# Loading the expert rows of u: four GpSimd gathers to all 128 partitions in place of four SyncE transfers to 32 partitions each

## The chip, the cores and the metric

The kernel runs on one core of one Trainium2 chip. The metric is the device time of one launch in microseconds (us), taken as the median of three runs. The core has TensorE for matrix products, VectorE (DVE in the profile), ScalarE (ACT), GpSimd (POOL) and SyncE (SP), which only issues transfers. Transfers run on 16 DMA engines, whichever engine issued them.

## The reference, cut to what matters

One decoder layer works on 512 tokens of width 2048. It has a token mixer (a convolution group and a differential attention group) and then a feed-forward part made of 16384 experts with one neuron each. Each token picks 16 experts in each of 8 heads by two scores. The expert part is:

```python
def apply(args):
    xb, ib, gb = args
    u = jnp.take(expert_u, ib, axis=0)
    a = jnp.einsum('thkd,td->thk', u, xb)
    w = (jax.nn.gelu(a.astype(jnp.float32), approximate=False) * gb).astype(xb.dtype)
    vv = jnp.take(expert_v, ib, axis=0)
    return jnp.einsum('thk,thkd->td', w, vv)
```

expert_u and expert_v are 16384 x 2048 in float32, 128 MB each. All else of the layer (projections, attention, the selection of experts) comes before this part.

## The kernel before, in words

The kernel splits the 512 tokens. 352 of them (TD) are computed densely: every expert's activation is computed for every token, and a gate matrix that is zero for experts not chosen is multiplied in. The other 160 (TG) are computed sparsely: for each token the chosen rows of expert_u and expert_v are gathered, one row to a partition.

The dense part runs over 128 blocks of 128 experts. `u_load` (L497 to L500) brings a block of expert_u, 128 rows of 8 KB, into a tile `ur` of 128 partitions by 4 by 512. Partition 32 s + r holds, in place b, the 2 KB segment s of row 32 b + r. It does so by four transfers of SyncE, one for each s, each to 32 partitions. This layout lets VectorE turn the block in squares of 32 by 32 (`utf`, L767, two halves to a block). Each half is split in a rounded part (ScalarE, L88) and a remainder (VectorE, L89) into `ut`, and TensorE multiplies it with the dense tokens (`pa`, L779). `ur` has two buffers (UR_BUFS), `utf` and `ut` two each. The tile is asked for one half-block ahead (AHEAD).

Eight blocks make a chunk. After the u side of a chunk comes its v side, `v_group`: tiles `vr` of expert_v, 512 KB each, loaded by SyncE (L922, three buffers), split by L88 and L89 into `vs`, and multiplied with the gated activations W (`pv`, L932). Results are added into `acc`.

Woven into both sides are the gathers of the sparse part: `gathered` (L829 to L836) issues an indirect DMA of GpSimd (L831) that fetches half a row of 4 KB for each of 128 partitions into `gt` (four buffers, GBUF). VectorE multiplies and sums it (L840 for u, L856 for v). There are 640 gathers. Each also waits for a recent matmul (`pace`), so that the gathers follow TensorE.

A scheduler in the tool chain lays down the order of instructions on each engine at compile time from readiness and program order; at run time each engine works through its own list in order, and the semaphores hold it.

Before the dense part, in the output projection (L505 to L548), the first 12 blocks (NPRE) are loaded by the same `u_load` into `uar` (two buffers), turned and stored in DRAM in turned form, one block to every second step of weights. In that stage GpSimd computes the remainders of the weights (`wsp`, L89 with the engine given as GpSimd). These 12 blocks come back later by plain transfers (L760) that the change doesn't touch. So `u_load` runs 128 times: 12 for `uar`, 116 for `ur`.

Of the kernel before, what the change touches and what calls it, by code (L numbers as in the profile page):

```python
# [14 lines left out]
U32 = mybir.dt.uint32  # L15
# [7 lines left out]
P = 128  # L23
T = 512
D = 2048
# [53 lines left out]
def hymba_peer(tc, x, c, positions, w_ada, b_ada, norm1_g, w_in, conv_w, q_norm_g, k_norm_g,  # L79
               lambda_q1, lambda_k1, lambda_q2, lambda_k2, subln_g, w_out, norm2_g,  # L80
               w_peer_q, sub_keys1, sub_keys2, expert_u, expert_v, out):
    nc = tc.nc
    x, out = x[0], out[0]
    w_ada, w_in, w_out, w_peer_q = w_ada[0], w_in[0], w_out[0], w_peer_q[0]
    expert_u, expert_v = expert_u[0], expert_v[0]
# [12 lines left out]
    with ExitStack() as ctx:  # L98
        const = ctx.enter_context(tc.tile_pool(name="const", bufs=1))
# [6 lines left out]

        ident = const.tile([P, P], F32, name="ident")
        make_identity(nc, ident)
        modc = const.tile([P, 6, KC], F32, name="modc")
        big_ctx = ctx.enter_context(ExitStack())  # L110
        early = big_ctx.enter_context(tc.tile_pool(name="early", bufs=1))
# [23 lines left out]
        def px():  # L135
            return psX.tile([P, T], F32, name="px")
# [358 lines left out]
        x1 = []  # L495

        def u_load(t, e):  # L497
            for s in range(4):
                nc.sync.dma_start(t[s * 32:(s + 1) * 32],
                                  expert_u[e * P:(e + 1) * P, s * 512:(s + 1) * 512].rearrange("(b r) d -> r b d", r=32))  # L500

        def u_quarter(t, ur, q):
            nc.vector.transpose(t, ur[:, :, q * P:(q + 1) * P].rearrange("p b (c r) -> p c b r", r=32))
# [2 lines left out]
        def u_ahead(e):  # L506
            ur = pu.tile([P, 4, 512], F32, name="uar")
            u_load(ur, e)
            t = pu.tile([P, 4, 4, 4, 32], F32, name="uat", bufs=PU_BUFS)
            for q in range(4):  # L510
                u_quarter(t[:, q], ur, q)
            nc.sync.dma_start(u_dram[e], t.rearrange("p q c b r -> p (q c b r)"))
# [3 lines left out]
        for dg in range(4):  # L516
            xr = xy.tile([P, NT, 512], F32, name="xr")
            nc.sync.dma_start(xr, x[:, dg * 512:(dg + 1) * 512].rearrange("(i p) d -> p i d", p=P))
            for j in range(4):
                t = px()  # L520
# [50 lines left out]
        for k in range(KC):  # L571
            xs = x1[k]
            t = nc.vector.scalar_tensor_tensor(xs, xs, a_col[:, 1, k:k + 1], rst, op0=OP.mult, op1=OP.mult)
# [17 lines left out]
        for i, kk in enumerate((sub_keys1, sub_keys2)):  # L591
            kr = tk.tile([P, P], F32, name="kr", bufs=1)
            nc.sync.dma_start(kr, kk[0])
            t = px()
# [158 lines left out]
        def u_turn(n):  # L753
            e, q = divmod(n, 2)
            if e >= NK:
                return
            if q == 0:
                UR[0] = up.tile([P, 4, 512], F32, name="ur", bufs=UR_BUFS)
                if e < NPRE:
                    nc.sync.dma_start(UR[0].rearrange("p b d -> p (b d)"), u_dram[e])  # L760
                else:
                    u_load(UR[0], e)
            if e < NPRE:
                t = UR[0][:, 2 * q:2 * q + 2].rearrange("p a (c b r) -> p (a c) b r", c=4, b=4)
            else:
                t = up.tile([P, 8, 4, 32], F32, name="utf", bufs=UTF_BUFS)
                nc.vector.transpose(t, UR[0][:, :, q * 256:(q + 1) * 256].rearrange("p b (c r) -> p c b r", r=32))  # L767
            UT[n] = up.tile([P, 2, 8, P], F32R, name="ut", bufs=UT_BUFS)
            split(UT[n], t.rearrange("p c b r -> p c (b r)"))
# [229 lines left out]
        for ch in range(nch):  # L999
            for b in range(CH):  # L1000
                e = ch * CH + b
# [40 lines left out]
```

## Time and profile before

| | before |
|---|---|
| median of 3 runs | 3594.22 us (3593.55 to 3598.7) |
| the profiled execution | 3579.26 us, its span 3577.3 us |
| TensorE busy | 3244.6 us, 91% of the span |
| VectorE busy | 2893.8 us, 81% |
| GpSimd busy | 1424.5 us, 40% |
| ScalarE busy | 1222.2 us, 34% |
| moved by DMA | 896.25 MB, mean 251 GB/s |
| granted clock of TensorE, mean | 0.964 |

The page divides the span in 40 slices of 89 us. The dense part proper fills the slices from about the twentieth to the thirty-eighth. A stretch in microseconds is counted from the span's start. In the page and in the answers a queue with the letter q0 (software_dynamic) is that of GpSimd's transfers and q1 (hardware_dynamic) that of SyncE's.

### The profile page before, as it was taken

The page shows a single profiled execution, that of the slowest core. Times are in us where ns is not written, and L with a number is a line of the kernel's source. Part 1 is how long each engine was busy: PE and PEld are TensorE (multiplying, and loading weights), DVE is VectorE, ACT ScalarE, POOL GpSimd, SP SyncE. Part 2 cuts the span into 40 slices and gives each one's busy share as a digit, 9 for nine tenths or more (in the row PEclk, how much of TensorE's full clock was granted, in tenths as well). Part 3 has the DMA queues.
Part 4 walks back from the last instruction along what each step waited for, and adds up shares of the span by engine and source line. Part 5 has one row for each costly group of instructions (what it writes and reads, how often), then busy time and mean ns, then how long its engine had stood idle before and what let it go on. Part 6 is the DMA issues. An engine that isn't in the chain of part 4 may idle for free.

```text
span 3577.3 us, 48356 instructions
## 1 busy us (share of the span) xinstructions
PE 3244.6 (91%) x18006; PEld 2982.2 (83%) x18006; DVE 2893.8 (81%) x4261; ACT 1222.2 (34%) x1827; POOL 1424.5 (40%) x985
## 2 busy tenths in 40 slices
PE   4788999999999888899999999999999999999985
PEld 3666877677787787899999899999999999999985
DVE  6999776752349999778888888888988898988885
ACT  4223343343255357422223222232333233222222
POOL 2346422344436620135444443444344343434441
PEclk9898999999999999999999999999999999999997
DMA  7774756658932135789999999999999999999985
GB/s 253 236 255 124 241 190 195 218 162 244 285 97 72 64 127 200 236 279 312 305 311 311 288 309 305 286 312 303 307 298 304 293 307 312 288 315 309 284 301 183
DMA packets 417513, 896.25 MB, mean 251 GB/s; under 512 B 32209, under 2 KB 110974, under 8 KB 412542
## 3 DMA queue, kind: packets, MB, share of 16 engines
q1 hardware_dynamic: 325118, 557.59, 53.1%
q0 software_dynamic: 92160, 335.59, 27.7%
q8 instruction: 141, 2.31, 0.3%
q14 instruction: 94, 0.77, 0.1%
HBM read 843.47 MB, written 49.55 MB: 250 GB/s over the span
## 4 chain that ended last, share of the span: by engine, by line
DMA 34%; DVE 31%; PE 17%; issue 12%; POOL 4%; SPq 1%; ACT 1%; DVEq 0%; POOLq 0%; ACTq 0%
DMA gt<-in_expert_v_dram,idxu 10%; DMA gt<-in_expert_u_dram,idxu 6%; DVE ada_acc L188 6%; DMA ur<-in_expert_u_dram 6%; PE pm L446 5%; DMA ada_w<-in_w_ada_dram 4%; POOL gt L831 3%; PE pa L779 2%; DVE gacc L856 2%; DVE utf L767 2%; DVE gt L840 2%; DVE ut L89 2%; DVE vs L89 2%; PE pv L932 2%; DVE gt L894 2%
## 5 line engine op out<-in xcount | busy, mean ns | idle before, releaser
L932 PE MATMUL pv<-W,vs 128*128 128x352 f32 x6144 | 1078.0, 329 | 84.2 <-DVE vs L89 58.5
L779 PE MATMUL pa<-hd,ut 128*128 128x352 f32 x6144 | 1080.8, 328 | 51.5 <-DVE ut L89 46.2
L932 PEld LDWEIGHTS pv<-W,vs 128*128 128x128 f32 x6144 | 1015.7, 192 | 100.5 <-DVE vs L89 69.9
L779 PEld LDWEIGHTS pa<-hd,ut 128*128 128x128 f32 x6144 | 1018.1, 192 | 63.3 <-DVE ut L89 55.3
L89 POOL TENSOR_TENSOR wsp<-wraw,wsp 128x1024 fp32r<-128x1024 f32 x160 | 396.4, 2480 | 588.8 <-ACT wsp L88 539.6
L831 POOL DMA_INDIRECT gt<-in_expert_u_dram,idxu x256 | 337.0, 1316 | 639.9 <-DVE gt L840 306.2
L88 ACT ACTIVATE vs<-vr 128x1024 fp32r<-128x1024 f32 x256 | 271.2, 1060 | 799.9 <-PE pv L932 408.9
L831 POOL DMA_INDIRECT gt<-in_expert_v_dram,idxu x256 | 346.4, 1353 | 480.9 <-DVE gacc L856 315.2
L856 DVE SCALAR_TENSOR_TENSOR gacc<-gt,ga_a,gacc 128x1024 f32<-128x1024 f32 x316 | 400.5, 1280 | 111.9 <-DMA gt<-in_expert_v_dram,idxu 83.1
L840 DVE SCALAR_TENSOR_TENSOR gt<-gt,h2n 128x1024 f32<-128x1024 f32 x320 | 386.2, 1218 | 123.5 <-DMA gt<-in_expert_u_dram,idxu 94.8
L188 DVE SCALAR_TENSOR_TENSOR ada_acc<-ada_w,scol,ada_acc 128x512 f32<-128x512 f32 (+1 forms) x390 | 387.1, 996 | 56.4 <-DMA ada_w<-in_w_ada_dram 48.9
L88 ACT ACTIVATE ut<-utf 128x1024 fp32r<-128x1024 f32 x232 | 244.6, 1056 | 275.3 <-DVE utf L767 152.5
L89 DVE TENSOR_TENSOR vs<-vr,vs 128x1024 fp32r<-128x1024 f32 x256 | 310.0, 1211 | 19.9 <-ACT vs L88 19.9
L767 DVE STREAM_TRANSPOSE utf<-ur 128x1024 f32<-128x1024 f32 x232 | 287.4, 1240 | 12.8 <-DMA ur<-in_expert_u_dram 7.2
L88 ACT ACTIVATE wsp<-wraw 128x1024 fp32r<-128x1024 f32 x160 | 169.0, 1058 | 371.5 <-issue 92.4
L89 DVE TENSOR_TENSOR ut<-utf,ut 128x1024 fp32r<-128x1024 f32 x232 | 282.2, 1218 | 9.1 <-ACT ut L88 9.1
L446 PE MATMUL pm<-big,wsp 128*128 128x512 f32 x1152 | 285.6, 400 | 0.0
L446 PEld LDWEIGHTS pm<-big,wsp 128*128 128x128 f32 x1152 | 214.1, 191 | 42.2
L237 PE MATMUL pqk<-wsp,big 128*128 128x512 f32 x768 | 201.8, 422 | 30.2 <-DVE qk L282 25.0
L237 PEld LDWEIGHTS pqk<-wsp,big 128*128 128x128 f32 x768 | 154.7, 205 | 69.3 <-DVE qk L282 30.3
L688 PE MATMUL pm<-big,wsp 128*128 128x512 f32 x768 | 186.7, 400 | 11.9 <-POOL wsp L89 10.3
L534 PE MATMUL pm<-big,wsp 128*128 128x512 f32 x768 | 181.5, 396 | 7.2 <-DVE x L540 7.2
(271 smaller groups left out, 3057.2 us busy)
## 6 DMA issues: line engine op xcount, KB each, us to landing
vr<-in_expert_v_dram SPq DMA_DIRECT2D x256, 512.0 KB
ur<-in_expert_u_dram SPq DMA_DIRECT2D x464, 256.0 KB
ada_w<-in_w_ada_dram SPq DMA_DIRECT2D x192, 512.0 KB
wraw<-in_w_in_dram SPq DMA_DIRECT2D x96, 512.0 KB
g_dram<-gtile SPq DMA_DIRECT2D x11, 2048.0 KB
g<-g_dram SPq DMA_DIRECT2D x32, 704.0 KB
wraw<-in_w_out_dram SPq DMA_DIRECT2D x32, 512.0 KB
wraw<-in_w_peer_q_dram SPq DMA_DIRECT2D x32, 512.0 KB
```

Of the source, the lines that this page charges most:

```text
L88: hi = nc.scalar.activation(dst[:, 0], src, AF.Copy)
L89: (eng or nc.vector).tensor_tensor(out=dst[:, 1], in0=src, in1=dst[:, 0].bitcast(F32), op=OP.subtract)
L188: nc.vector.scalar_tensor_tensor(acc, wt[:, k], s, acc, op0=OP.mult, op1=OP.add)
L237: nc.tensor.matmul(banks[i], hT[kk][:, a, i * P:(i + 1) * P], ws[:, b, k], start=(kk == last[0] and n == 0), stop=(kk == last[1] and n == 2))
L446: nc.tensor.matmul(banks[n2], ws[:, a, k, n2 * P:(n2 + 1) * P], hT[kk][:, b], start=(kk == 0 and n == 0), stop=(kk == KC - 1 and n == 2))
L688: nc.tensor.matmul(banks[j], ws[:, a, k, j * P:(j + 1) * P], h2T[kk][:, b], start=(kk == 0 and n == 0), stop=(kk == KC - 1 and n == 2))
L767: nc.vector.transpose(t, UR[0][:, :, q * 256:(q + 1) * 256].rearrange("p b (c r) -> p c b r", r=32))
L779: mm = nc.tensor.matmul(pa[:, :TD], ut[:, a, j], hd[k][:, b], start=(k == 0 and n == 0), stop=(k == KC - 1 and n == 2))
L831: d = nc.gpsimd.indirect_dma_start(out=t, out_offset=None, in_=src, in_offset=bass.IndirectOffsetOnAxis(ap=gidx[g][:, j:j + 1], axis=0), e ...
L840: nc.vector.scalar_tensor_tensor(t, t, 1.0, h2n[:, f * D // 2:(f + 1) * D // 2], op0=OP.mult, op1=OP.mult, accum_out=ga_a[:, f, j:j + 1])
L856: nc.vector.scalar_tensor_tensor(gacc[:, s], t, a, gacc[:, s], op0=OP.mult, op1=OP.add)
L932: mm = nc.tensor.matmul(pv[j // 2][:, j % 2, :TD], vs[:, a, bb, j * P:(j + 1) * P], W[e0 // 2][:, m, bb], start=(b == 0 and n == 0), stop= ...
```

## The change

The loading of a block is moved from SyncE to GpSimd, as four indirect DMAs, one for each b. The table expert_u is seen as rows of 2 KB (`u_rows`). A constant index column `uidx` of one number for each partition, made once at the start by four iotas, holds s + 4 r in partition 32 s + r, and the offset of the block and of b is a constant of each instruction. Each gather writes place b of all 128 partitions, 2 KB in each. The bytes, their places in the tile and all that follows the load stay the same.

```diff
+        u_rows = expert_u.rearrange("n (s d) -> (n s) d", s=4)
+        uidx = const.tile([P, 1], U32, name="uidx")
+        for s in range(4):
+            nc.gpsimd.iota(uidx[s * 32:(s + 1) * 32], pattern=[[0, 1]], base=s, channel_multiplier=4,
+                           allow_small_or_imprecise_dtypes=True)
...
         def u_load(t, e):
-            for s in range(4):
-                nc.sync.dma_start(t[s * 32:(s + 1) * 32],
-                                  expert_u[e * P:(e + 1) * P, s * 512:(s + 1) * 512].rearrange("(b r) d -> r b d", r=32))
+            for b in range(4):
+                nc.gpsimd.indirect_dma_start(out=t[:, b], out_offset=None, in_=u_rows,
+                                             in_offset=bass.IndirectOffsetOnAxis(ap=uidx, axis=0),
+                                             element_offset=(e * P + b * 32) * D)
```

## Rows read from the trace of the kernel before

**Rows 1.** The page: busy time of each engine over the span, and the line of the DMA engines' busy tenths in 40 slices.
```profile
PE 3244.6 (91%) x18006; PEld 2982.2 (83%) x18006; DVE 2893.8 (81%) x4261; ACT 1222.2 (34%) x1827; POOL 1424.5 (40%) x985
...
DMA  7774756658932135789999999999999999999985
```

**Rows 2.** The view by stretches, main stage, 1700 to 3412 us. Columns: length; busy us (and instructions) of PE, PEld, DVE, ACT and POOL; granted clock; share of the 16 DMA engines; GB/s.
```profile
1700.00:3412.00 1712.00, 1623.56 (x9801) 1602.03 (x9801) 1504.72 (x1619) 503.24 (x564) 719.27 (x539) 0.98 1.01 303
```

**Rows 3.** The DMA view of the main stage: packets and bytes, and the issues of expert_u's blocks by SyncE.
```profile
DMA packets 228967, 518.79 MB, mean 303 GB/s; under 512 B 18911, under 2 KB 55519, under 8 KB 228591
...
ur<-in_expert_u_dram SPq DMA_DIRECT2D x411, 256.0 KB
```

**Rows 4.** The chain of waits near 2430 us: start, length, what. An unbroken run of 24 matmuls.
```profile
2427.77 3.87 PE pv L932 x24
```

**Rows 5.** The waits of the main stage: who waited for whom, us in total, times, longest.
```profile
ACT vs L88 <- DMA vr<-in_expert_v_dram: 287.2, 60, 10.4
...
PE pv L932 <- DVE vs L89: 48.7, 30, 5.4
...
PE pa L779 <- DVE ut L89: 24.3, 18, 4.5
```

**Rows 6.** The waits of DVE alone in the main stage, same columns.
```profile
DVE gacc L856 <- DMA gt<-in_expert_v_dram,idxu: 83.1, 72, 4.8
DVE gt L840 <- DMA gt<-in_expert_u_dram,idxu: 70.3, 60, 5.1
...
DVE utf L767 <- DMA ur<-in_expert_u_dram: 6.9, 5, 3.3
```

**Rows 7.** The waits of POOL alone in the main stage, same columns.
```profile
POOL gt L831 <- DVE gacc L856: 347.3, 163, 6.1
POOL gt L831 <- DVE gt L840: 345.5, 155, 6.5
```

**Rows 8.** The chain of waits: pieces in which a gather was awaited, from its start to its arrival. Three of the main stage (two shown), then five after the last u transfer was issued at 3412.6 us (three shown).
```profile
2489.42 11.46 DMA gt<-in_expert_v_dram,idxu
...
2533.20 9.59 DMA gt<-in_expert_v_dram,idxu
...
3443.36 8.04 DMA gt<-in_expert_v_dram,ib
...
3505.44 6.25 DMA gt<-in_expert_v_dram,ib
...
3513.83 5.20 DMA gt<-in_expert_v_dram,ib
```

**Rows 9.** The timeline of SyncE's queue, 2610 to 2640 us: start, length, line, what, how many in a row.
```profile
2611.18 2.74 SPq L499 DMA_DIRECT2D ur<-in_expert_u_dram  x4
2615.08 8.56 SPq L922 DMA_DIRECT2D vr<-in_expert_v_dram  x2
2625.21 1.75 SPq L499 DMA_DIRECT2D ur<-in_expert_u_dram  x4
```

**Rows 10.** The DMA view of two short stretches: above the line of dots 2616.6 to 2619 us, below it 2625.5 to 2628.6 us. Queue lines: packets, MB, share of 16 engines.
```profile
DMA packets 319, 0.57 MB, mean 237 GB/s; under 512 B 37, under 2 KB 62, under 8 KB 319
...
q1 hardware_dynamic: 297, 0.51, 97.8%
q0 software_dynamic: 22, 0.06, 10.8%
...
DMA packets 438, 1.27 MB, mean 409 GB/s; under 512 B 32, under 2 KB 32, under 8 KB 438
...
q0 software_dynamic: 236, 0.87, 69.6%
q1 hardware_dynamic: 202, 0.40, 33.2%
```

**Rows 11.** The groups of POOL in the main stage: count, busy us, mean ns of one, idle before.
```profile
L831 POOL DMA_INDIRECT gt<-in_expert_v_dram,idxu x256 | 346.4, 1353 | 480.9 <-DVE gacc L856 315.2 <-DMA gt<-in_expert_v_dram,idxu 67.8 <-issue 27.7
L831 POOL DMA_INDIRECT gt<-in_expert_u_dram,idxu x191 | 250.7, 1313 | 336.0 <-DVE gt L840 253.6 <-issue 33.9 <-PE pa L779 24.4
L831 POOL DMA_INDIRECT gt<-in_expert_u_dram,ib x64 | 83.4, 1303 | 121.9 <-DVE gt L840 79.1 <-issue 19.1 <-PE pa L779 13.8
L831 POOL DMA_INDIRECT gt<-in_expert_v_dram,ib x28 | 38.8, 1384 | 53.8 <-DVE gacc L856 23.9 <-DVE gacc L854 12.2 <-PE pa L779 8.0
```

**Rows 12.** The timeline of DVE and POOL in three places: start, length, engine, line, what, [idle before <- what ended it].
```profile
2611.85 1.27 DVE L856 SCALAR_TENSOR_TENSOR gacc<-gt,ga_a,gacc 128x1024 f32<-128x1024 f32 x1
...
2613.39 0.94 POOL L831 DMA_INDIRECT gt<-in_expert_v_dram,idxu  x1 [2.18 <-DVE gacc L856]
...
2660.88 1.19 DVE L89 TENSOR_TENSOR vs<-vr,vs 128x1024 fp32r<-128x1024 f32 x1
2660.93 1.96 POOL L831 DMA_INDIRECT gt<-in_expert_v_dram,idxu  x1 [0.30 <-issue]
...
3505.44 0.94 POOL L831 DMA_INDIRECT gt<-in_expert_v_dram,ib  x1 [0.30 <-issue]
```

**Rows 13.** The waits of SyncE's own queue in the main stage (columns as in rows 5).
```profile
SPq L499 <- DVE utf L767: 428.3, 90, 13.3
```

**Rows 14.** The view by stretches (columns as in rows 2): the output projection while the first 12 blocks are loaded.
```profile
834.00:960.00 126.00, 118.80 (x535) 98.14 (x535) 44.87 (x66) 35.61 (x48) 52.74 (x24) 0.97 1.04 314
```

**Rows 15.** The group of POOL's weight remainders in the same stretch (columns as in rows 11).
```profile
L89 POOL TENSOR_TENSOR wsp<-wraw,wsp 128x1024 fp32r<-128x1024 f32 x21 | 50.7, 2417 | 73.6 <-ACT wsp L88 73.6
```

## The prediction

> **What bounds the kernel now.** I read the page first. The DMA engines show nines from the nineteenth slice on, TensorE is busy 91% and GpSimd 40% [rows 1]. So the stage to read is the dense expert part. There 1712 us hold 411 / 4 = 102.75 blocks of u [rows 2, 3], 16.66 us to a block, and all 116 blocks of `ur` are priced by it below. Within 0.2% (7 us) is what I count as no change, about what a measurement of this kernel can tell.
>
> Per block each resource needs, at the least:
> - TensorE: 9801 / 102.75 = 95.4 matmuls [rows 2] at 3.87 / 24 = 0.161 us [rows 4], 15.4 us. The waits that it shows are for remainders of VectorE, 48.7 + 24.3 = 73 us, 0.7 us a block [rows 5].
> - VectorE: 1504.72 / 102.75 = 14.6 us, 88% [rows 2]. Of its waits, 153 us are for gathers and only 6.9 us for `ur` [rows 6].
> - GpSimd: 539 / 102.75 = 5.25 gathers [rows 2]. It idles more than it works, and 347.3 + 345.5 = 693 us of that it waits for VectorE to free a `gt` buffer [rows 7]. So the gathers go round a loop of four buffers, one turn in 4 x 16.66 / 5.25 = 12.7 us. A turn is the issue, the arrival, VectorE's use of it and the restart.
> - DMA: 518.79 / 102.75 = 5.05 MB [rows 3], at a share of 1.01 [rows 2].
>
> The arrival is the long part of that turn: 9.59 to 11.46 us from a gather's start [rows 8]. The DMA view says why. After four u transfers were issued [rows 9] there is a stretch at 237 GB/s in which SyncE's queue holds 97.8% of the engines' time and the gathers move 0.06 MB; some 9 us later the same engines move 409 GB/s, with the gathers at 0.87 MB [rows 10]. At 0.51 MB in 2.4 us a block of u (1.05 MB) takes 4.9 us, in which the gathers nearly stand still. The other 4.0 MB at 409 GB/s take 9.8 us, so 14.7 us a block at the least. I read this stage as a loop of gathers lengthened by DMA, with TensorE and VectorE close behind.
>
> **The change part by part.** *DMA, gained.* If a gather of u to all partitions flows like the other gathers, a block's 5.05 MB need 12.3 us instead of 14.7, and the gathers no longer stand still for 4.9 us. What they then cost is shown after the last u transfer: five awaited gathers arrived in 5.20 to 8.04 us, the middle one in 6.25 [rows 8]. I take 6.25, since the load there is gathers and v transfers, as it would be. The Trainium skill (SBUF — State Buffer, Door 1: The DMA port swizzle) states that a transfer to partitions 0 to 31 reaches half of the 16 SBUF ports and measured 189 GB/s against 328 with all partitions, at 1 MiB. The trace agrees in kind, with 237 against 409 GB/s [rows 10]; by that rule alone the change is a gain, which is the first rival.
>
> *GpSimd, paid.* 4 indirect DMAs a block are added to 5.25. One takes (346.4 + 250.7 + 83.4 + 38.8) / 539 = 1.33 us [rows 11], and the next begins 0.30 us after its end at the earliest [rows 12]: 1.63 us. The trace shows no gather of 2 KB rows; an index still goes to each of 128 partitions, so I price it like the 4 KB ones. Its ends are 0.94 + 0.30 = 1.24 and 1.96 + 0.30 = 2.26 us [rows 12]. A gather takes 0.94 us beside L856 or with VectorE idle, and 1.96 us where L89 starts just ahead of it. SyncE's issues cost VectorE and GpSimd nothing. The Trainium skill speaks against the move (SBUF — State Buffer, SBUF: two separate sides): VectorE in a two-port mode keeps GpSimd from writing descriptors, and it advises the issue from SP or ACT. The trace shows such a delay beside L89 and not beside L856; at 0.94 us each instead of 1.33 the four would cost 1.6 us a block less.
>
> So GpSimd needs 9.25 x 1.63 = 15.1 us a block where it needed 8.6 (ends 11.5 and 20.9). It works in order, so what counts is what queues behind what. SyncE's rows have the four u transfers in a row [rows 9], as all four become free with one tile, and I expect the same on GpSimd. Queued behind them is the next gather, and VectorE waits for that. A block then goes: four u gathers, 6.5 us; four gathers into free buffers; the fifth must wait until the first has arrived (6.25 from its start), VectorE has got to it (0.6, half an operation, as VectorE is 88% busy), has used it (1.28) and GpSimd has restarted (2613.39 - 2611.85 - 1.27 = 0.27) [rows 8, 12]. The fifth starts at 6.52 + 6.25 + 0.6 + 1.28 + 0.27 = 14.92, and 1.25 gathers of 1.63 end at 16.96 us. That is 0.30 us over today's 16.66, x 116 = +35 us. Its ends: with arrival 5.20 and no wait 15.3, below TensorE's 15.4, so 15.4 a block or -146 us; with arrival 8.04 18.75, or +242 us.
>
> *u later.* A block's last issue comes 4.9 us after its first instead of 1.75 to 2.74 [rows 9], and behind gathers. Price 0: VectorE waits for `ur` only 6.9 us in all [rows 6]; if that cover were gone it is the third rival.
>
> *SyncE, emptied.* Its queue stands 428.3 us at the head of u loads [rows 13], with v loads behind. These now come earlier. ScalarE waits 287.2 us for `vr`, but TensorE only 48.7 us for what follows [rows 5], and in VectorE's order that stands behind gathers too. Price 0, at best -49.
>
> *Output projection.* 12 blocks put 48 gathers on GpSimd. It has 52.74 us of work in 24 instructions [rows 14]; with 0.30 for each and 48 x 1.24 (no L89 of VectorE there) it comes to 119 of 126 us. Four take 5.0 us; GpSimd now idles 73.6 / 20 = 3.7 us ahead of a remainder [rows 15], so 1.3 us stick out, 16 us in all at 12 blocks. I take half, +8. Ends: -7, TensorE's whole idle time there (126 - 118.8 [rows 14]), since the loads compete for a DMA share of 1.04; and +60, with nothing covered.
>
> *Index.* Four iotas at the start, before anything needs them, on an engine that is 40% busy [rows 1]: 0, at most four gathers' 6.5 us.
>
> Sum: 35 + 8 = +43 us. On the profiled execution, 3579.26 becomes 3622. Its time lies 15 us under the median of the three runs, 3594.22, on which I forecast: 3637.
>
> **The rivals.** *Faster: DMA was the bound, and GpSimd fits.* The scheduler sets gathers between the u gathers, so no burst forms; GpSimd's 15.1 us then lie under TensorE's 15.4. For it: the arrival time and the 237 GB/s. Against it: GpSimd is then at 95% and in order. At 16.0 us a block, TensorE with most of its waits kept, -0.66 x 116 = -77: 3517, within 3470 to 3585. It decides as soon as the fifth gather starts before 14.6 us in my sum.
>
> *No change.* A 4.9 us standstill in DMA is exchanged for a 6.5 us standstill in GpSimd's queue, while arrival shortens by 3.3 us or more: they cancel, 3594 within 7.
>
> *Much slower: the buffer wait comes in line.* SyncE's 428.3 us wait for a free `ur` [rows 13] is harmless there. On GpSimd gathers stand behind it. With half of it paid, 214 + 43: 3851. It decides if GpSimd reaches a u gather well before VectorE's turn of the block two before. Against it: a GpSimd at over 90% comes late, not early.
>
> *It doesn't do what it says.* The slow stretch may come from the source (2 KB pieces 8 KB apart), which stays. Then arrival stays 9.59 and a block takes 20.3 us: +422, about 4020.
>
> **How the numbers follow.** The forecast, slower by the loop on GpSimd, 0.40, with a range of its own of 3602 to 3720. Faster 0.38, no change 0.11, buffer wait 0.07, no gain in DMA 0.04. So faster 0.38, same 0.11, slower 0.51. The range of 3490 to 3770 leaves out the low end of the first rival (some 0.06) and the last two (0.11); the +242 and +60 ends lie above it in part, as they need every block at its worst.
>
> **What would show it.** Right: no stretch near 237 GB/s, a DMA share near 0.8 in the main stage, gathers arriving in about 6 us, GpSimd busy about 70% (9.25 x 1.33 of 17 us) with runs of four u gathers and its waits for VectorE shrunk, VectorE's waits for gathers grown. If GpSimd's waits shrink and VectorE's do too, the first rival holds. If the list on GpSimd mixes both kinds, the burst in my sum is wrong. Long waits of u gathers for L767 show the third rival, arrivals near 10 us the last.

## The result and the profile after

| | before | after |
|---|---|---|
| median | 3594.22 us (3593.16 to 3604.09, 5 runs) | 3635.79 us (3622.51 to 3641.22, 5 runs) |
| after / before | | 1.0112, 95% interval 1.0095 to 1.0129 |
| the profiled execution, its span | 3579.26 us, 3577.3 us | 3630.96 us, 3629.0 us |

The change makes the kernel 41.6 us slower by the medians, 51.7 us by the spans of the two profiled executions, which is what the rows below can account for.

The page of the kernel after: busy time of the engines, and the DMA engines' tenths in 40 slices.

```profile
PE 3252.7 (90%) x18006; PEld 2989.5 (82%) x18006; DVE 2908.2 (80%) x4261; ACT 1225.3 (34%) x1827; POOL 2084.4 (57%) x1501
...
DMA  7774756658722134788888888888888888988885
```

Against [rows 1] the nines of the DMA line have become eights, but for one, from the nineteenth slice on, and GpSimd went from 40% to 57%. TensorE has the same 18006 matmuls in more time.

The view by stretches of the kernel after, output projection and main stage, columns as in rows 2.

```profile
834.00:960.00 126.00, 123.91 (x572) 101.72 (x571) 53.48 (x71) 39.03 (x51) 99.75 (x73) 1.00 0.91 326
...
1700.00:3412.00 1712.00, 1604.84 (x9630) 1585.05 (x9629) 1467.83 (x1588) 498.02 (x555) 1231.30 (x928) 0.97 0.87 294
```

In the main stage TensorE got through 9630 matmuls where it had got through 9801 [rows 2], 171 fewer in the same 1712 us. At 1712 / 9630 = 0.178 us each that is 30 us. The DMA share fell from 1.01 to 0.87, and fewer bytes moved in a second (294 against 303 GB/s): DMA is not what holds the stage any more. GpSimd is busy 1231.30 / 1712 = 72%.

The waits of POOL and then of DVE in the main stage, kernel after: us in total, times, longest.

```profile
POOL gt L837 <- issue: 131.7, 339, 3.9
POOL ur L504 <- issue: 102.0, 331, 0.5
POOL gt L837 <- DVE gacc L862: 76.6, 46, 5.0
POOL gt L837 <- DVE gt L846: 56.0, 28, 5.4
POOL ur L504 <- DVE utf L773: 27.5, 45, 3.3
```

```profile
DVE gt L846 <- DMA gt<-in_expert_u_dram,idxu: 101.2, 55, 5.2
DVE gacc L862 <- DMA gt<-in_expert_v_dram,idxu: 85.9, 50, 5.6
DVE gt L846 <- DMA gt<-in_expert_u_dram,ib: 41.5, 18, 8.4
```

GpSimd waited 693 us for VectorE to free a buffer [rows 7], now 133 us. VectorE's waits for gathers went the other way, from 153 us in the two rows of [rows 6] to 187 us in their successors, and the longest from 5.1 to 8.4 us. So the idle time has moved from ahead of GpSimd to ahead of VectorE: GpSimd now comes late.

The timeline of POOL, kernel after, one block of u near the middle of the main stage: start, length, engine, line, what, [idle before <- what ended it].

```profile
2618.47 1.67 POOL L504 DMA_INDIRECT ur<-in_expert_u_dram,uidx  x1 [0.51 <-DVE utf L773]
2620.44 0.95 POOL L504 DMA_INDIRECT ur<-in_expert_u_dram,uidx  x1 [0.30 <-issue]
2621.70 1.21 POOL L504 DMA_INDIRECT ur<-in_expert_u_dram,uidx  x1 [0.30 <-issue]
2623.22 1.96 POOL L504 DMA_INDIRECT ur<-in_expert_u_dram,uidx  x1 [0.30 <-issue]
2625.48 0.94 POOL L837 DMA_INDIRECT gt<-in_expert_v_dram,idxu  x1 [0.30 <-issue]
2626.73 1.69 POOL L837 DMA_INDIRECT gt<-in_expert_v_dram,idxu  x1 [0.30 <-DVE ge L817]
2628.73 0.94 POOL L837 DMA_INDIRECT gt<-in_expert_v_dram,idxu  x1 [0.30 <-issue]
2629.97 0.94 POOL L837 DMA_INDIRECT gt<-in_expert_v_dram,idxu  x1 [0.30 <-issue]
2633.15 1.68 POOL L837 DMA_INDIRECT gt<-in_expert_v_dram,idxu  x1 [2.24 <-DVE gacc L862]
2635.44 0.95 POOL L504 DMA_INDIRECT ur<-in_expert_u_dram,uidx  x1 [0.61 <-DVE utf L773]
```

The timeline of DVE beside it, same kernel and columns.

```profile
2626.33 1.27 DVE L862 SCALAR_TENSOR_TENSOR gacc<-gt,ga_a,gacc 128x1024 f32<-128x1024 f32 x1
2627.53 1.21 DVE L89 TENSOR_TENSOR ut<-utf,ut 128x1024 fp32r<-128x1024 f32 x1
2631.60 1.28 DVE L862 SCALAR_TENSOR_TENSOR gacc<-gt,ga_a,gacc 128x1024 f32<-128x1024 f32 x1 [2.86 <-DMA gt<-in_expert_v_dram,idxu]
```

The block reads like the prediction's sum. Four u gathers stand in a row, 7.0 us. The gather behind them is the one that VectorE wants: it starts at 2625.48, and VectorE, idle for 2.86 us, takes it up at 2631.60. Meanwhile GpSimd has put three more gathers in the three other buffers and stops; the fifth starts when VectorE has freed the first, 14.7 us after the block's first u gather. The next block begins at 2635.44, 17.0 us after this one.

The DMA view of 2600 to 2640 us, a digit (busy tenths of the 16 engines) and a rate for each microsecond; first the kernel before, below the dots the kernel after.

```profile
DMA  9999999999999999999999999999999999999999
GB/s 176 174 209 352 356 367 367 336 394 388 364 381 400 400 392 364 228 244 227 229 330 305 254 217 313 369 410 416 401 279 221 242 215 250 289 322 297 344 340 324
...
DMA  9999996798998777999998999599999999999999
GB/s 395 387 291 360 406 416 191 180 283 324 397 385 295 266 186 234 346 395 344 391 393 332 363 369 399 219 248 283 305 345 316 286 363 387 401 411 333 396 395 414
```

Before, the engines are full throughout, and yet the rate falls to 174 to 254 GB/s again and again. After, where they are full (a nine) no microsecond falls below 248 GB/s, and the lower rates (180 to 234) stand where the engines are not full. Behind the four u gathers of the block shown the rate is 332 to 399 GB/s (2621 to 2625 us).

### The profile page after: what moved, and what is told of

The parts are those of the page before. It is cut to its first block, busy times and chain, and to the rows that moved or that the text cites. A ratio compares the mean times of both kernels' runs of the same rounds, so it can differ in the third digit from the quotient of the medians.

```text
span 3629.0 us, 48408 instructions
## 1 busy us (share of the span) xinstructions
PE 3252.7 (90%) x18006; PEld 2989.5 (82%) x18006; DVE 2908.2 (80%) x4261; ACT 1225.3 (34%) x1827; POOL 2084.4 (57%) x1501
## 5 line engine op out<-in xcount | busy, mean ns | idle before, releaser
L785 PE MATMUL pa<-hd,ut 128*128 128x352 f32 x6144 | 1092.4, 330 | 65.6 <-DVE ut L89 52.3
L504 POOL DMA_INDIRECT ur<-in_expert_u_dram,uidx x464 | 643.8, 1387 | 310.4 <-DVE utf L773 138.7
L89 POOL TENSOR_TENSOR wsp<-wraw,wsp 128x1024 fp32r<-128x1024 f32 x160 | 394.1, 2468 | 520.9 <-ACT wsp L88 477.8
L846 DVE SCALAR_TENSOR_TENSOR gt<-gt,h2n 128x1024 f32<-128x1024 f32 x320 | 386.2, 1217 | 187.3 <-DMA gt<-in_expert_u_dram,idxu 139.8
L862 DVE SCALAR_TENSOR_TENSOR gacc<-gt,ga_a,gacc 128x1024 f32<-128x1024 f32 x316 | 402.0, 1281 | 120.4 <-DMA gt<-in_expert_v_dram,idxu 85.9
L837 POOL DMA_INDIRECT gt<-in_expert_v_dram,idxu x256 | 329.4, 1287 | 172.2 <-DVE gacc L862 75.9
L89 DVE TENSOR_TENSOR vs<-vr,vs 128x1024 fp32r<-128x1024 f32 x256 | 309.5, 1209 | 16.6 <-ACT vs L88 13.5
L89 DVE TENSOR_TENSOR ut<-utf,ut 128x1024 fp32r<-128x1024 f32 x232 | 281.4, 1215 | 8.8 <-ACT ut L88 8.6
L451 PE MATMUL pm<-big,wsp 128*128 128x512 f32 x1152 | 287.7, 402 | 0.0
L773 DVE STREAM_TRANSPOSE utf<-ur 128x1024 f32<-128x1024 f32 x232 | 286.4, 1236 | 0.1
L694 PE MATMUL pm<-big,wsp 128*128 128x512 f32 x768 | 187.8, 402 | 15.5 <-POOL wsp L89 13.9
```

The costliest lines, as they stand in the source:

```text
L89: (eng or nc.vector).tensor_tensor(out=dst[:, 1], in0=src, in1=dst[:, 0].bitcast(F32), op=OP.subtract)
L451: nc.tensor.matmul(banks[n2], ws[:, a, k, n2 * P:(n2 + 1) * P], hT[kk][:, b], start=(kk == 0 and n == 0), stop=(kk == KC - 1 and n == 2))
L504: nc.gpsimd.indirect_dma_start(out=t[:, b], out_offset=None, in_=u_rows, in_offset=bass.IndirectOffsetOnAxis(ap=uidx, axis=0), element_off ...
L785: mm = nc.tensor.matmul(pa[:, :TD], ut[:, a, j], hd[k][:, b], start=(k == 0 and n == 0), stop=(k == KC - 1 and n == 2))
L837: d = nc.gpsimd.indirect_dma_start(out=t, out_offset=None, in_=src, in_offset=bass.IndirectOffsetOnAxis(ap=gidx[g][:, j:j + 1], axis=0), e ...
L846: nc.vector.scalar_tensor_tensor(t, t, 1.0, h2n[:, f * D // 2:(f + 1) * D // 2], op0=OP.mult, op1=OP.mult, accum_out=ga_a[:, f, j:j + 1])
```

## The experiments

Each kernel was timed against the kernel before on the same chip; the ratio has its 95% interval. The kernel before had medians of 3584 to 3594 us on the chips used, so kernels are compared by their ratios. To see the main stage apart from the rest, the table also counts the matmuls between 1700 and 3300 us in each profiled execution (view by stretches) and turns them into a time for one block: 1600 x 95.4 / matmuls, with the prediction's 95.4 matmuls to a block.

| kernel | median, us | ratio to before | matmuls 1700 to 3300 | us a block |
|---|---|---|---|---|
| before | 3594.22 | 1 | 9173 | 16.64 |
| after | 3635.79 | 1.0112 (1.0095 to 1.0129) | 9014 | 16.93 |
| 1: SyncE to 128 partitions | 3428.04 | 0.9562 (0.951 to 0.9615) | 9922 | 15.38 |
| 2: plain transfers by GpSimd | 3625.56 | 1.0105 (1.0049 to 1.0162) | 9063 | 16.84 |
| 3: first 12 blocks by SyncE | 3629.45 | 1.0129 (1.0072 to 1.0186) | 9068 | 16.83 |
| 4: every second block by SyncE | 3641.89 | 1.0174 (1.0112 to 1.0237) | 8931 | 17.09 |
| 5: u gathers tied between gathers | 3934.52 | 1.0966 (1.0907 to 1.1026) | 7680 | 19.88 |
| 6: as 5, without the tie | 3627.8 | 1.0103 (1.0072 to 1.0135) | 9012 | 16.94 |
| 7: after, five gather buffers | 3519.54 | 0.9808 (0.9771 to 0.9846) | 9427 | 16.19 |
| 8: before, five gather buffers | 3609.86 | 1.0058 (1.0036 to 1.008) | 8968 | 17.02 |
| 9: before, SyncE's order changed | 3546.09 | 0.9892 (0.9848 to 0.9936) | 9383 | 16.27 |
| 10: before, halves by SyncE and ScalarE | 3516.55 | 0.981 (0.9774 to 0.9845) | 9533 | 16.01 |
| 11: before, all by ScalarE | 3606.49 | 1.0046 (1.0026 to 1.0067) | 9113 | 16.75 |
| 12: 10 with five gather buffers | 3540.39 | 0.9863 (0.9833 to 0.9893) | 9275 | 16.46 |

### 1. The partitions alone: SyncE's four transfers, each to all 128

```diff
-            for s in range(4):
-                nc.sync.dma_start(t[s * 32:(s + 1) * 32],
-                                  expert_u[e * P:(e + 1) * P, s * 512:(s + 1) * 512].rearrange("(b r) d -> r b d", r=32))
+            for b in range(4):
+                nc.sync.dma_start(t[:, b], expert_u[e * P:(e + 1) * P, b * 512:(b + 1) * 512])
```

> The kernel before, with each of the four SyncE transfers of a block going to all 128 partitions (2 KB pieces, 8 KB apart in the source, as before). The rows land in other partitions than the computation needs, so the u side multiplies misplaced numbers; the amount of work is the same. Theory A (32 partitions make the u transfers slow; GpSimd's queue is what the change pays): the relief comes without the price. A turn of the gather loop falls from 12.7 us towards 6.25 + 0.6 + 1.28 + 0.27 = 8.4 us, TensorE's 15.4 us a block and its waits bound the stage at about 16.0, so about 3594 - 77 = 3517, ratio 0.98, no stretch near 237 GB/s, DMA share below 0.9. Theory B (the source's short pieces make them slow): nothing changes, ratio 0.995 to 1.005, DMA share stays 1.0.

Measured 0.9562. The view by stretches of this kernel, columns as in rows 2:

```profile
1700.00:3300.00 1600.00, 1597.91 (x9922) 1597.03 (x9921) 1515.95 (x1626) 506.92 (x570) 742.15 (x546) 1.00 0.93 327
```

TensorE is busy 1597.91 of 1600 us: the stage is TensorE's, at the 15.4 us a block that the prediction had worked out as its least. VectorE's largest waits for gathers are 13.5 and 9.6 us, where [rows 6] had 83.1 and 70.3. The source is read in the same 2 KB pieces 8 KB apart, so the standstill of the gathers before came from the 32 partitions at the receiving end. What the change takes away is thus worth some 156 us by itself, and what it puts on GpSimd costs more than that: after stands at 1.0112 / 0.9562 = 1.058 of this kernel.

### 2. GpSimd alone: the old transfers, issued there

```diff
-                nc.sync.dma_start(t[s * 32:(s + 1) * 32],
+                nc.gpsimd.dma_start(t[s * 32:(s + 1) * 32],
```

> The kernel before, with its four transfers to 32 partitions each issued by GpSimd instead of SyncE, as plain transfers. Theory A: GpSimd's price without the relief. With arrivals at 9.59 us the burst sum gives 20.3 us a block, so well above the changed kernel: 3700 to 4020, DMA share about 1.0, if a plain transfer costs GpSimd about what a gather does (1.33 us; no row shows that). Theory B (no relief in the change at all): like the changed kernel, 3620 to 3650.

Measured 1.0105. The groups of POOL of this kernel, 1700 to 3300 us: count, busy us, mean ns of one, idle before.

```profile
L499 POOL DMA_DIRECT2D ur<-in_expert_u_dram x384 | 221.5, 593 | 80.7 <-DVE utf L767 64.0 <-DVE gacc L856 6.3 <-DMA ur<-in_expert_u_dram 3.8
```

A plain transfer occupies GpSimd for 0.593 us, the change's gather for 1.38, so this kernel added less than half of the burst. It kept the slow arrival: the gathers awaited in the chain of waits of the main stage took 10.5 us at the median (10.4 before), and the DMA share between 1700 and 3300 us is 0.98. It lost about as much as the change did, the number of theory B, whose reason (no relief in the change) run 1 has refuted; the large loss that was expected from a burst of the full size on top of slow arrivals was not put to the test.

### 3. The first 12 blocks by SyncE again

```diff
         def u_load(t, e):
+            if e < NPRE:
+                for s in range(4):
+                    nc.sync.dma_start(t[s * 32:(s + 1) * 32],
+                                      expert_u[e * P:(e + 1) * P, s * 512:(s + 1) * 512].rearrange("(b r) d -> r b d", r=32))
+                return
```

> The changed kernel, with the 12 early blocks (uar, output projection) loaded by SyncE again. By the forecast the early blocks cost 8 us, so 3636 - 8 = 3628. The trace of the changed kernel shows TensorE busy 123.9 of 126 us there against 118.8 before, which says that they gained about 5: then 3641. Either way within 10 us of the changed kernel, the loss lies in the main stage. If most of the 42 us of loss goes away (below 3605), the loss was in the output projection or in its order.

Measured 1.0129, no better than after. The loss does not lie in the output projection.

### 4. Every second block by SyncE

```diff
         def u_load(t, e):
+            if e % 2:
+                for s in range(4):
+                    nc.sync.dma_start(t[s * 32:(s + 1) * 32],
+                                      expert_u[e * P:(e + 1) * P, s * 512:(s + 1) * 512].rearrange("(b r) d -> r b d", r=32))
+                return
```

> The changed kernel, with the odd blocks loaded by SyncE as before. Theory A: relief and price are both halved, but the price comes from a full queue, which 7.25 x 1.63 = 11.8 us a block no longer fills, so the sum turns: 3550 to 3590, faster than both. Rival (the price is proportional to the number of u gathers, as a fixed cost each): half of the way, about 3615.

Measured 1.0174, with GpSimd busy only 892.25 of 1600 us (56%). The gain expected from a half-relieved GpSimd did not come, and the kernel is slower than half of the way too: a fifth less of GpSimd's occupation bought nothing. Half of the relief is gone with it, though, so this run alone doesn't tell the occupation from the burst; run 7 does. VectorE's waits for gathers are as in the kernel after (102.5 + 99.4 + 20.7 us between 1700 and 3300 us). It fits that each block pays for its own kind of standstill, slow arrivals in one and a burst in the next, but this was not shown by itself.

### 5 and 6. Taking the burst apart by order

The u gathers are written one at a time between the steps of the block before. In 5 each is also tied behind the last sparse gather; 6 leaves out the tie and nothing else.

```diff
+        def u_begin(e):
...
+            UN[e] = up.tile([P, 4, 512], F32, name="ur", bufs=UR_BUFS)
...
+                waiting.extend((UN[e], e, b) for b in range(4))
...
+        def u_feed():
+            if waiting:
+                d = u_piece(*waiting.pop(0))
+                if gathers:
+                    tc.add_manual_dep(d.ins, gathers[-1].ins.name, ORDER, reason="one between the gathers")
...
+                    if j % 4 == 3:
+                        u_feed()
```

> The changed kernel, with the four u gathers of a block set one by one behind gathers of the sparse part in GpSimd's order (asked for half a block earlier, each with an order edge to the last gather). The number of instructions on every engine is the same. Theory A (the cost is the run of four in front of a loop of four buffers): without the run a block is bounded by GpSimd's 9.25 x 1.63 = 15.1 us and TensorE's 15.4, so 15.5 to 16.2 us instead of 16.98, or 80 to 150 us off the changed kernel: 3490 to 3560. Rival (what costs is GpSimd's total, wherever its work stands): 3620 to 3650 as before.

5 measured 1.0966, far from the gain that was hoped for. The four did not come apart one by one either: in GpSimd's list of the main stage they stand mostly as one and three, and ten times 22 or 23 sparse gathers follow each other. Its waits of POOL and then of PE, 1700 to 3300 us, columns as in rows 5:

```profile
POOL gt L861 <- PE pv L963: 313.9, 104, 7.2
```

```profile
PE pa L805 <- ACT ut L88: 140.4, 14, 14.7
```

GpSimd waits 313.9 us for matmuls, where the kernel after had 15.8 us of that wait. Each sparse gather waits for a recent matmul (`pace`); a u gather tied behind one waits with it; and TensorE in turn waits for what is made of u, up to 14.7 us at a time. The tie closed a ring.

```diff
                 d = u_piece(*waiting.pop(0))
-                if gathers:
-                    tc.add_manual_dep(d.ins, gathers[-1].ins.name, ORDER, reason="one between the gathers")
```

> The changed kernel with its u gathers written one at a time into the program between the steps of the block before, as in the run 0.097 slower, but without the forced place behind the last sparse gather. Theory A (that run lost because u gathers were tied behind sparse gathers that wait for TensorE's pace, so that TensorE waited for u and u for TensorE): without the tie the loss goes, 3560 to 3650. Theory B (it lost because the u gathers are asked for early and hold up the queue whatever the tie): 3800 or more.

6 measured 1.0103: without the tie the loss is gone, and so is the interleaving. The timeline of POOL of this kernel:

```profile
2618.99 1.67 POOL L503 DMA_INDIRECT ur<-in_expert_u_dram,uidx  x1 [0.51 <-DVE utf L789]
2620.97 0.95 POOL L503 DMA_INDIRECT ur<-in_expert_u_dram,uidx  x1 [0.30 <-issue]
2622.23 0.96 POOL L503 DMA_INDIRECT ur<-in_expert_u_dram,uidx  x1 [0.30 <-issue]
2623.49 1.96 POOL L503 DMA_INDIRECT ur<-in_expert_u_dram,uidx  x1 [0.30 <-issue]
2625.76 0.95 POOL L859 DMA_INDIRECT gt<-in_expert_v_dram,idxu  x1 [0.30 <-issue]
```

The scheduler lays the four in a row again, though they are written apart: in the main stage all 103 groups of this kernel stand so, as 102 do in the kernel after. No kernel here breaks up the burst and does nothing else, so what the burst costs by itself stays argued.

### 7 and 8. The loop itself: a fifth gather buffer

To make room, `vr` goes from three buffers to two. 7 is this edit on the kernel after, 8 the same on the kernel before.

```diff
-GBUF = 4
+GBUF = 5
...
-VR_BUFS = 3
+VR_BUFS = 2
```

> The changed kernel with five gt buffers instead of four; for room, two vr buffers instead of three. Theory A: the fifth gather of a block no longer waits for the first, 6.52 + 5.25 x 1.63 = 15.1 us, TensorE's 15.4 takes over, so 3500 to 3570, if two vr buffers cost little (ScalarE waited only 11 us for vr in the changed kernel). Rival (GpSimd's total): 3620 to 3650.

> The kernel before with five gather buffers instead of four, paid for with two buffers of vr instead of three: the control to the same edit of the changed kernel, which ran at 0.981 of before. Theory A (the loop of four buffers is what GpSimd's bursts lengthen; before, the loop is lengthened by slow arrivals in the same way): the fifth buffer gives before something too, 0.98 to 0.99 of before, so that the changed kernel with five buffers is no better than this one by over 0.5%. Theory B (the loop binds the changed kernel alone, and before waits for DMA bytes): before with five buffers stays within 0.5% of before or loses by the missing vr buffer, and the change is then worth 2% once five buffers are there.

7 measured 0.9808, by the ratios some 110 us under the kernel after. Its waits of DVE, 1700 to 3300 us:

```profile
DVE gt L846 <- DMA gt<-in_expert_u_dram,idxu: 69.1, 48, 3.5
DVE gacc L862 <- DMA gt<-in_expert_v_dram,idxu: 28.2, 26, 3.8
```

The burst is still there (104 groups of four in GpSimd's list), GpSimd is busy 1240.31 of these 1600 us where it was 1146.91, and most of the price is gone: with a fifth buffer GpSimd goes on while the first gather is on its way. That is the loop of the prediction, opened, so it is not GpSimd's occupation that sets the price. The `vr` buffer that was given up can only have hidden a part of the gain: ScalarE's wait for v is 200.3 us here and 11.0 in the kernel after.

8 measured 1.0058. Its waits of ACT and then of DVE, 1700 to 3300 us:

```profile
ACT vs L88 <- DMA vr<-in_expert_v_dram: 574.9, 101, 18.5
```

```profile
DVE vs L89 <- ACT vs L88: 155.7, 58, 9.3
DVE gt L840 <- DMA gt<-in_expert_u_dram,idxu: 27.2, 26, 4.6
```

The waits for gathers shrink here too (27.2 us and less, from 83.1 and 70.3), but the missing `vr` buffer takes their place: ScalarE waits 574.9 us for v, twice the 285.8 of the kernel before in the same stretch, as v loads still stand in SyncE's queue behind u loads. In 7 they don't. The gain that theory A named did not come, and the number is that of theory B (a loss by the missing `vr` buffer). Its reason, that the loop of four binds the changed kernel alone and the kernel before waits for DMA bytes, is not settled: the waits would shrink if the loop was opened, and they would also shrink because VectorE now waits elsewhere; and the DMA share is still 1.00, where 7 has 0.90. A fifth buffer with three `vr` buffers was not run.

### 9, 10 and 11. The ports without GpSimd

9 changes the order of SyncE's four transfers; 10 gives partitions 64 to 127 to ScalarE's queue; 11 gives all four to ScalarE's queue in the old order.

```diff
-            for s in range(4):
+            for s in (0, 2, 1, 3):
```

```diff
-                nc.sync.dma_start(t[s * 32:(s + 1) * 32],
+                (nc.sync if s < 2 else nc.scalar).dma_start(t[s * 32:(s + 1) * 32],
```

```diff
-                nc.sync.dma_start(t[s * 32:(s + 1) * 32],
+                nc.scalar.dma_start(t[s * 32:(s + 1) * 32],
```

> The kernel before, with the four SyncE transfers of a block in the order of partitions 0, 64, 32, 96 instead of 0, 32, 64, 96. If transfers of one queue overlap at their ends and halves matter, a small gain, 3540 to 3580; if one queue's transfers pass one after the other, nothing, within 0.3% of before.

> The kernel before, with the transfers to partitions 0 to 63 issued by SyncE and those to 64 to 127 by ScalarE. Same four transfers, no GpSimd. If the 32 partitions limit a transfer, and transfers of the two queues to different halves flow side by side, much of the gain of sp128 comes here with the right result: 3430 to 3540, if ScalarE's in-order wait for a free ur costs little. If transfers of the two queues don't flow side by side: 3570 to 3600. If ScalarE's wait hurts: above 3600.

> The kernel before with its four u transfers to 32 partitions each, in their old order, issued by ScalarE's queue instead of SyncE's. SyncE's queue is emptied of u loads as in the changed kernel, v loads stand behind none, and neither the ports nor GpSimd are touched. Theory A (splitting the load over two queues gained 1.9% because both halves of the partitions were fed at once): here the gathers still stand still, 0.993 to 1.01 of before. Theory B (that run, and part of what the change gains, came from v loads no longer queued behind u loads that wait for a buffer): 0.975 to 0.988, near that run.

Measured 0.9892, 0.981 and 1.0046. Merely alternating between the partitions below 64 and those above gains 1.1%; feeding both halves from two queues gains 1.9%; emptying SyncE's queue without it gains nothing, though ScalarE's wait for `vr` falls from 285.8 to 177.5 us between 1700 and 3300 us. So which partitions are written at one time matters by itself (9, in one queue), and the gain of 10 is put down to the same; a split over two queues that keeps both in one half of the partitions was not run. The Trainium skill (SBUF — State Buffer, "Can I just issue two DMAs to hit both halves?") answers its question with no: two transfers at partitions 0 and 64 measured only 6% over one. In this kernel 32-partition transfers spread over both halves are a gain, 1.1 and 1.9% of the whole time, so here the measurement decides. No run times two such transfers alone; what shrinks in 10 is VectorE's waits for the gathers beside them, to 49.3 and 43.9 us from 70.3 and 83.1.

### 12. The two gains together

On top of 10:

```diff
-GBUF = 4
+GBUF = 5
...
-VR_BUFS = 3
+VR_BUFS = 2
```

> The kernel before with partitions 0 to 63 of each u block loaded by SyncE and 64 to 127 by ScalarE's queue, and with five gather buffers and two vr buffers. Theory A (the loop of gathers is still the bound when both halves of the ports are fed at once): 0.96 to 0.97 of before, near the 3428 us of the kernel whose SyncE transfers reach all partitions. Theory B (with the ports relieved TensorE is the bound and the buffers add nothing): 0.978 to 0.985, as with four buffers.

Measured 0.9863, outside both ranges, though its interval reaches into that of theory B, and slower than 10 alone. VectorE now waits 104.2 us for `vs` from ScalarE, as in 8: with u loads still in SyncE's queue two `vr` buffers are too few. Run 1 aside, whose rows are misplaced, 7 and 10 are the fastest, both 2% under the kernel before and equal within their intervals.

## Why the prediction came out as it did

Forecast 3637 us, measured 3635.79. By its own steps:

*What bounds the kernel before.* Right as far as run 1 goes. It removed the slow arrivals and left a stage that TensorE fills, at 15.38 us a block against the 15.4 worked out. With quick arrivals four buffers are enough there. Whether with slow ones it was the loop or the full DMA engines that held the kernel before is open: run 8, which gave it a fifth buffer, lost a `vr` buffer too.

*DMA, gained.* Right in kind, and as a single term too small. In the slices of the DMA view above none with full engines lies below 248 GB/s, and the share is 0.87 where about 0.8 was named. The gathers awaited in the chain of waits took 10.4 us at the median before (58 pieces of the main stage) and 6.9 us after (41 pieces, from 2252 us on, where the chain begins); 6.25 was taken. Pieces of this chain, kernel after, start, length, what:

```profile
2355.02 11.20 DMA gt<-in_expert_v_dram,idxu
...
2608.01 5.23 DMA gt<-in_expert_v_dram,idxu
...
2625.48 6.02 DMA gt<-in_expert_v_dram,idxu
```

What the relief is worth without GpSimd's part, 156 us (run 1), is twice the 77 us of the faster rival, which let TensorE keep most of its waits; it lost nearly all of them. The 4.9 us of slow DMA for a block of u were too few as well: in the view above six of the eight slices from 2616 to 2624 us run at 217 to 254 GB/s before the next u transfers are issued.

*GpSimd, paid.* Right. The groups of POOL, kernel after, main stage:

```profile
L504 POOL DMA_INDIRECT ur<-in_expert_u_dram,uidx x410 | 566.5, 1382 | 145.3 <-issue 102.0 <-DVE utf L773 27.5 <-DVE gacc L862 5.3
L837 POOL DMA_INDIRECT gt<-in_expert_v_dram,idxu x256 | 329.4, 1287 | 172.2 <-DVE gacc L862 75.9 <-issue 52.5 <-DMA gt<-in_expert_v_dram,idxu 13.9
```

A gather of 2 KB rows takes 1.38 us, one of 4 KB rows 1.29: pricing by the index and not by the bytes held (1.33 taken). The run of four forms, the fifth gather starts 14.7 us into the block shown (14.92 in the sum), and the main stage takes 1712 x 95.4 / 9630 = 16.96 us a block, the figure forecast. Counted by u gathers instead (410 in the stretch) it would be 16.7: these run ahead of TensorE, so the matmuls are the better clock. From the first to the last u load the kernel before takes 2066.7 us and the kernel after 2098.0, which is 31 us more and agrees with the 35 of the sum. That the loop and not GpSimd's occupation sets the price is shown by run 7 (one buffer more, more occupation, some 110 us less). Not told apart is how much of the longer turn is the four issue times and how much u's bytes, which now go through the same DMA queue (q0) as the gathers.

One reading in this term was wrong, without weight in the sum. The gather of [rows 12] begins after L856 has ended, so it does not show that L856 leaves gathers alone. In the kernel after, the gather at 2626.73 us begins 0.40 us behind the start of an L862, the same operation, and takes 1.69 us; the 24 gathers of that kernel that begin 0.2 to 0.4 us behind one take 1.74 us at the median. The delay is not L89's alone.

*u later.* Right: VectorE's waits in the main stage hold none for `ur`.

*SyncE, emptied.* Right. ScalarE's wait for `vr`, 287.2 us before, is 11.0 us, and run 11 shows that the emptied queue alone gains nothing. It seems to matter in a way the prediction did not have: with two `vr` buffers ScalarE waits 200.3 us for v in 7, where the queue is empty of u, and 574.9 us in 8.

*Output projection.* Mis-sized, and the mechanism failed: +8 was forecast. In that stretch TensorE gained 123.91 - 118.80 = 5.1 us, near the end of -7, and GpSimd's 48 gathers fitted in. It was given back in the steps after: by 1700 us 7503 matmuls had been done against 7522 before, 3 us.

*What the sum left out.* The sparse gathers finish later. In the main stage 518 of their 640 were issued, against 539 [rows 2], and what remains runs when the dense blocks end: the last one starts at 3565.4 us, 117.6 us behind the last u load, where it was 3513.8 us and 101.3 us before. Of the 51.7 us between the two spans, 30 lie in the main stage and 3 ahead of it, so some 19 us lie after 3412 us. The forecast of +43 (35 for the main stage and 8 for the output projection) thus stands between 41.6 by the medians and 51.7 by the spans. The 8 that did not come and the 19 that were left out went opposite ways, so that it hit the median to 1.2 us is in part luck.

*The rivals.* The faster one fell because its condition was not met: the scheduler sets no gathers between the u gathers, and forcing it (5) closes a ring. Its number, 3517, is near what run 7 gives (3519.54) once the fifth gather hardly waits. The buffer wait in line is 27.5 us, not 214: as argued, GpSimd comes late to it. That the change brings no relief in DMA is refuted by run 1 and by the arrivals (10.4 to 6.9 us). No change came near: two effects of some 150 and 200 us did nearly cancel, but not within 0.2%.

## What to carry to other kernels

Moving a transfer to another queue moves its issue time too: price it on the new engine, in order, with all four issues in a row, and follow what stands behind them until the next buffer must come back. When a ring of buffers sets the pace, look at its depth before its speed: one buffer more was worth some 110 us here, and the change that lost 1.1% then won 1.9%. Before paying an engine for a better spread over the partitions, try the same spread by order or by a second idle queue.

## What the runs showed that had not been expected

- An indirect gather occupies GpSimd for 1.38 us on average (0.94 to 1.96 in the block shown), a plain transfer of the same block for 0.593 us.
- Four transfers of 32 partitions cost the kernel 1.1% less in the order 0, 64, 32, 96 than in the order 0, 32, 64, 96.
- SyncE's four transfers to 128 partitions let the stage run at a granted clock of 1.00 where it was 0.98 before and 0.97 after: TensorE without pauses was granted its full 2.4 GHz throughout.
- A gather's occupation hangs on what VectorE is doing. In the kernel after, gathers that begin in the first 0.2 us of an L846 or an L89 on VectorE take some 1.97 us at the median; beside the turning of u (L773) they take 0.94.
- Two buffers of `vr` cost little when v loads have a queue to themselves (run 7: VectorE waits 15.8 us for ScalarE's `vs`) and much when u loads stand ahead of them (155.7 us in 8, 104.2 in 12).
